# Where in a step the transpose of a finished attention output is issued

## The chip, the cores and the metric

The kernel runs on one core of a Trainium2 chip. The metric is the time of one execution on the device, in microseconds; lower is better. One core has TensorE (matrix products and transposes, into PSUM banks), VectorE, ScalarE, GpSimd and SyncE, which here issues all the DMAs. Each engine works through its own queue in order.

## What is computed

One layer of an encoder on 1024 tokens of width 1024, in 32-bit floats:

```python
h = rmsnorm(x)
[qA|kA|vA|qB|kB|vB|gA|gB] = h @ w_in
yA = differential attention (4 heads, rotary, block-causal mask), each head's output normalised
yB = chunked band attention (8 heads, own chunk and 8 before, learned bias)
x += (sigmoid(gA) * (yA @ w_up_a) + sigmoid(gB) * (yB @ w_up_b)) @ w_out
x += cross-attention to 256 memory tokens (4 heads)
x += SwiGLU(rmsnorm(x)); out = rmsnorm(x)
```

The change touches the attention phase alone, that is `yA`, `yB` and the gate products `gA`, `gB` that are mixed into it.

## The kernel before

Each product is made of three matmuls on split operands (a high and a low part): lines 217, 218 and 219 for the dense products that are mixed into the attention, lines 95 to 97 where a product stands alone. A split is a ScalarE cast (line 76) and a VectorE subtraction (line 81).

**The feed.** The dense products of the phase (the projections of queries, keys and values of later heads, and 32 gate jobs) lie in a queue, `feed`. A gate or query/key job is eight portions, each of three 512-wide matmuls and entered at 0.65 us; a value job is eight portions of three 256-wide matmuls, entered at 0.33. `feed.fill(us)` takes whole portions from the queue until their entries have used up `us`; `feed.need` runs jobs that must be done. A gate job ends with a ScalarE copy (line 257) and a store (line 258). What is left in the queue behind the attention is run by `feed.drain()`, after the loads of the next stage's operands have been issued.

**The attention.** There are 64 units: 32 of A (head `hi` 0 to 3, eight row blocks `b` each) and 32 of B (`hi` 4 to 7, two halves `c` of four block pairs `j` each). `s()` of a unit makes its scores (lines 312, 313) and softmax; it is called one unit ahead. A unit is then worked off in groups of up to four 128-wide blocks, one group in a step; there are 120 steps, 48 in A, 72 in B. A step fills, transposes the group's probabilities into the bank `tr` (A line 352, B line 438; `tr` has one buffer), splits them into `pt` out of that bank, and then multiplies the previous group's `pt` by V (`avs`, lines 366 and 367 in A, 454 in B). The last group's `avs` of a unit also finishes its output: in A it is normalised into `o`, in B added into `yt` (line 463).

**The end of a unit.** Two steps after its output is finished, `ends(2)` calls the unit's `end()`. In A that is one transpose of `o` into `tr` (line 384) and a ScalarE copy into `yt` (line 385), with a store of the whole head at the last block (line 387). In B it is only the store of a finished pair of heads (line 467).

**The next stage** loads the eight attention outputs (line 587), splits them, and multiplies by `w_up` (lines 95 to 97), gated by the sigmoid of the stored gates.

The order on each engine is laid out by the framework's planner: earlier in the program is earlier on the engine, unless the plan finds the instruction not ready and something later is.

Of the kernel before, what the change touches and what calls it, by code (L numbers as in the profile page):

```python
# [37 lines left out]
def build(tc, x, mem, wqk, wv, wg, wup, wout, wcq, wck, wcv, wco, wgu, wdn,  # L38
# [186 lines left out]
    feed = Feed()  # L225
# [4 lines left out]
    with tc.tile_pool(name="at", bufs=1, reuse_waits="tile") as at:  # L230
# [242 lines left out]
        for i in range(8):  # L473
            vj, v = vjs[i // 2]
            if i < 4:
                us = [UnitA(i, b, qks[i], v, vj) for b in range(NT)]
            else:
                us = [UnitB(i - 4, c, j, qks[i], v, vj) for c in range(2) for j in range(4)]
# [49 lines left out]
        def flush():  # L528
            nonlocal pend
            if pend:  # L530
                un, g, pt = pend
                pend = None
                un.avs(g, pt)
                if g == un.groups()[-1]:
                    ended.append((step, un))
# [3 lines left out]
        def ends(age):  # L539
            while ended and step - ended[0][0] >= age:  # L540
                ended.pop(0)[1].end()

        for n, (hi, u) in enumerate(flat):
            if u is heads[hi][0] and hi < 7:
                feed.first(*qks[hi + 1].jobs)
            if n + 1 < len(flat):
                nx = flat[n + 1][1]
                feed.need(*nx.pre_s)
                nx.s()
            if u is heads[hi][0] and hi % 2 == 0 and hi > 0:  # L550
                flush()
                feed.first(*vjs[hi // 2][0])
            gs = u.groups()
            for i, g in enumerate(gs):
                us = (FA if hi < 4 else FB) * u.weight / len(gs)
                step += 1
                feed.fill(us)
                ends(2)
                pt = u.tr(g)
                flush()  # L560
                if i == 0:
                    feed.need(*u.pre_t)
                pend = (u, g, pt)
# [699 lines left out]
```

## Time and profile before

| | us |
|---|---|
| median of three timed runs | 1790.8 (1789.49 to 1791.02) |
| the profiled execution | 1787.65 |
| its span, first to last instruction | 1785.8 |
| TensorE busy | 1743.1 |
| VectorE busy | 1085.4 |
| ScalarE busy | 765.6 |
| GpSimd busy | 516.0 |

The attention phase with the feed runs from about 76 to 645 us. A row of a view gives busy times, or for a single instruction its start and duration in us; a bracket at the end of a row tells how long the engine stood idle before it, and for what. TensorE counts as busy from a matmul's start to its modelled end, so busy times of pipelined matmuls overlap.

### The profile page before, as it was taken

The numbers are of one execution on the slowest core, as the hardware profiler recorded it, in microseconds if no ns is written. First come the engines' busy times: TensorE is split into PE (matmuls) and PEld (weight loads), VectorE is DVE, ScalarE is ACT, GpSimd is POOL, SyncE is SP. The second block draws the span as 40 slices with busy tenths as digits, with TensorE's granted clock in tenths as the row PEclk, the third lists the DMA queues.
The fourth block names the chain that finished last, engine by engine and source line by source line (L and its number), as shares of the span: only waits on it lengthen the run. The fifth ranks groups of instructions, "written<-read, shape, count | busy, mean of one in ns | idle before, by whom it ended". The sixth has DMA issues, their size and how long they took to land.

```text
span 1785.8 us, 23577 instructions
## 1 busy us (share of the span) xinstructions
PE 1743.1 (98%) x8836; PEld 1469.2 (82%) x8836; DVE 1085.4 (61%) x1497; ACT 765.6 (43%) x1425; POOL 516.0 (29%) x553
## 2 busy tenths in 40 slices
PE   7999999999999999999999999999999999999997
PEld 7778797898898888888888887778888888888886
DVE  6585666656766644435645545886676656655556
ACT  5354554545545544213542334453333333334343
POOL 3231213213323201200000001476766655400002
PEclk9999999999999999999999999999999999999999
DMA  5331313212222256412331113315645434587664
GB/s 193 103 93 66 102 47 104 65 60 61 68 85 63 76 195 233 156 62 86 116 118 49 58 59 135 125 71 195 253 163 191 165 142 174 215 283 193 195 192 139
DMA packets 75729, 229.79 MB, mean 129 GB/s; under 512 B 9184, under 2 KB 9440, under 8 KB 71776
## 3 DMA queue, kind: packets, MB, share of 16 engines
q1 hardware_dynamic: 75616, 228.30, 37.8%
q8 instruction: 69, 1.13, 0.3%
q14 instruction: 44, 0.36, 0.1%
HBM read 160.10 MB, written 55.57 MB: 121 GB/s over the span
## 4 chain that ended last, share of the span: by engine, by line
PE 65%; issue 3%; DVE 3%; ACT 1%; POOL 1%; DMA 1%; DVEq 0%; POOLq 0%; ACTq 0%
PE bk L903 11%; PE bk L904 11%; PE bk L902 11%; PE acc L217 5%; PE acc L218 5%; PE acc L219 5%; PE s L96 2%; PE s L95 2%; PE s L97 2%; PE s L217 2%; PE s L218 2%; PE s L219 2%; PE av L454 1%; PE tr L438 1%; PE av L95 0%
## 5 line engine op out<-in xcount | busy, mean ns | idle before, releaser
L218 PE MATMUL acc<-t,wsp 128*128 128x512 f32 (+1 forms) x704 | 270.5, 384 | 0.0
L217 PE MATMUL acc<-t,wsp 128*128 128x512 f32 (+1 forms) x704 | 270.5, 384 | 0.0
L219 PE MATMUL acc<-t,wsp 128*128 128x512 f32 (+1 forms) x704 | 270.4, 384 | 0.0
L902 PE MATMUL bk<-T,w 128*128 128x512 f32 x616 | 240.0, 390 | 2.2 <-ACT r L990 2.0
L903 PE MATMUL bk<-T,w 128*128 128x512 f32 x616 | 239.8, 389 | 1.3 <-DVE w L897 1.3
L904 PE MATMUL bk<-T,w 128*128 128x512 f32 x616 | 239.8, 389 | 0.4 <-DVE T L897 0.4
L897 DVE TENSOR_TENSOR w<-fr,w 128x512 fp32r<-128x512 f32 x132 | 142.9, 1115 | 69.5 <-ACT w L896 69.1
L81 DVE TENSOR_TENSOR wsp<-raw,wsp 128x1024 fp32r<-128x1024 f32 x98 | 122.1, 1246 | 74.1 <-ACT wsp L76 72.9
L76 ACT CAST wsp<-raw 128x1024 fp32r<-128x1024 f32 x96 | 100.7, 1049 | 124.8 <-PE s L219 50.2
L219 PEld LDWEIGHTS acc<-t,wsp 128*128 128x128 f32 x704 | 133.3, 189 | 25.2
L218 PEld LDWEIGHTS acc<-t,wsp 128*128 128x128 f32 x704 | 133.3, 189 | 23.0 <-DVE wsp L81 0.8
L217 PEld LDWEIGHTS acc<-t,wsp 128*128 128x128 f32 x704 | 133.3, 189 | 22.2
L897 DVE TENSOR_TENSOR do<-dr,do 128x1024 fp32r<-128x1024 f32 x77 | 96.5, 1260 | 78.3 <-ACT do L896 76.1
L902 PEld LDWEIGHTS bk<-T,w 128*128 128x128 f32 x616 | 115.6, 188 | 26.6 <-ACT r L990 2.4
L903 PEld LDWEIGHTS bk<-T,w 128*128 128x128 f32 x616 | 115.6, 188 | 25.5 <-DVE w L897 1.7
L904 PEld LDWEIGHTS bk<-T,w 128*128 128x128 f32 x616 | 115.6, 188 | 25.0 <-DVE T L897 0.9
L896 ACT CAST do<-dr 128x1024 fp32r<-128x1024 f32 x77 | 81.0, 1053 | 112.6 <-PE bk L904 98.6
L903 PE MATMUL bk<-do 128*128 128x512 f32 x308 | 120.0, 390 | 2.5 <-DVE do L897 2.5
L904 PE MATMUL bk<-do 128*128 128x512 f32 x308 | 119.8, 389 | 0.0
L217 PE MATMUL acc<-wsp,t 128*128 128x256 f32 (+1 forms) x368 | 118.3, 321 | 1.0 <-POOL wsp L80 1.0
L902 PE MATMUL bk<-do 128*128 128x512 f32 x308 | 119.0, 389 | 0.0
L219 PE MATMUL acc<-wsp,t 128*128 128x256 f32 (+1 forms) x368 | 116.8, 318 | 0.7 <-DVE wsp L81 0.7
(218 smaller groups left out, 3728.9 us busy)
## 6 DMA issues: line engine op xcount, KB each, us to landing
fr<-in_wgu SPq DMA_DIRECT2D x44, 512.0 KB, 5.3
ad<-r SPq DMA_DIRECT2D x22, 512.0 KB, 3.3
sd<-s SPq DMA_DIRECT2D x11, 1024.0 KB, 4.1
dw<-in_wdn SPq DMA_DIRECT2D x22, 512.0 KB, 5.4
wd<-dw SPq DMA_DIRECT2D x11, 1024.0 KB, 3.9
dr<-sd SPq DMA_DIRECT2D x44, 256.0 KB, 3.7
dr<-wd SPq DMA_DIRECT2D x44, 256.0 KB, 3.9
dr<-ad SPq DMA_DIRECT2D x33, 256.0 KB, 5.0
```

Of the source, the lines that this page charges most:

```text
L76: act.copy(out=hi, in_=src)
L81: lo_eng.tensor_tensor(out=lo, in0=src, in1=hi.bitcast(F32), op=ALU.subtract)
L95: pe.matmul(acc, lh, rh, start=(i == 0), stop=False)
L96: pe.matmul(acc, ll, rh, start=False, stop=False)
L217: pe.matmul(acc, lh, rh, start=(i == 0), stop=False)
L218: pe.matmul(acc, ll, rh, start=False, stop=False)
L219: pe.matmul(acc, lh, rl, start=False, stop=(i == n - 1))
L896: self.act.copy(out=hi, in_=src)
L897: self.dve.tensor_tensor(out=lo, in0=src, in1=hi.bitcast(F32), op=ALU.subtract)
L902: mm(acc, l[0], r[0], start=start, stop=False, skip_group_check=onto)
L903: mm(acc, l[1], r[0], start=False, stop=False, skip_group_check=onto)
L904: mm(acc, l[0], r[1], start=False, stop=stop, skip_group_check=onto)
```

## The change

The budget of a step's fill is handed out in two halves, and `ends(2)` stands between them.

```diff
                 us = (FA if hi < 4 else FB) * u.weight / len(gs)
                 step += 1
-                feed.fill(us)
+                feed.fill(us / 2)
                 ends(2)
+                feed.fill(us / 2)
                 pt = u.tr(g)
                 flush()
```

The budget is `FA` (5.5) or `FB` (3.8) times the unit's weight, over its number of groups. For A the weight is 0.3 + 1.2 (b + 1) / 8, for B 0.5, 0.9, 1.3 and 1.3 by `j`. The loop that it is given to:

```python
        def fill(self, us):
            while us > 0 and self.q:
                us -= self.step()
```

## Rows read from the trace of the kernel before

**Rows 1.** The page, part 1: busy us, share of the span, instructions.

```profile
PE 1743.1 (98%) x8836; PEld 1469.2 (82%) x8836; DVE 1085.4 (61%) x1497; ACT 765.6 (43%) x1425; POOL 516.0 (29%) x553
```

**Rows 2.** Stretches: length, then each engine's busy us, clock, DMA.

```profile
76.00:392.00 316.00, 307.18 (x1713) 262.83 (x1712) 208.85 (x423) 162.77 (x409) 79.52 (x135) 0.99 0.25 77
392.00:644.55 252.55, 249.01 (x1533) 218.03 (x1532) 163.99 (x317) 133.88 (x292) 74.21 (x124) 1.00 0.22 70
644.55:671.62 27.07, 27.07 (x122) 22.37 (x120) 12.41 (x11) 12.99 (x16) 0.00 (x0) 1.00 0.80 288
```

**Rows 3.** TensorE's waits in A and B: total us, times, longest us.

```profile
PE tr L352 <- ACT yt L385: 4.9, 7, 1.7
...
PE tr L438 <- DVE pt L81: 2.9, 5, 0.9
```

**Rows 4.** One end in order of time (TensorE and ScalarE): start, duration, instruction.

```profile
254.69 0.27 PE L384 MATMUL tr<-ident,o 128*128 128x128 f32 x1
255.49 0.26 ACT L385 COPY yt<-tr 128x128 f32<-128x128 f32 x1
255.80 0.66 PE L352 MATMUL tr<-ident,pp 128*128 128x128 f32 x4 [0.36 <-ACT yt L385]
```

**Rows 5.** Line 384, what its engine idled for before it: us, times.

```profile
  DVE pt L81: 0.4, 2
```

**Rows 6.** Last two groups, in order of time: transposes, and the subtract that frees the bank.

```profile
639.11 0.62 PE L438 MATMUL tr<-ident,pb 128*128 128x128 f32 x4
640.43 0.69 DVE L81 TENSOR_TENSOR pt<-tr,pt 128x512 fp32r<-128x512 f32 x1 [0.96 <-ACT pt L76]
642.24 0.49 PE L438 MATMUL tr<-ident,pb 128*128 128x128 f32 x3
643.32 0.56 DVE L81 TENSOR_TENSOR pt<-tr,pt 128x384 fp32r<-128x384 f32 x1 [2.20 <-ACT pt L76]
```

**Rows 7.** Line 218 on TensorE by stretch: length, busy us (matmuls), clock.

```profile
606.38:644.55 38.17, 13.35 (x34) 1.00 0.16 56
633.39:636.24 2.85, 1.17 (x3) 1.00 0.00 0
644.55:671.62 27.07, 15.57 (x40) 1.00 0.80 288
```

**Rows 8.** VectorE's groups, 606.38 to 644.55: times, busy us, mean ns, idle before.

```profile
L417 DVE TENSOR_TENSOR pb<-s,bt 128x640 f32<-128x640 f32 (+2 forms) x6 | 4.2, 747 | 0.2 <-PE s L313 0.2
L418 DVE TENSOR_REDUCE mx<-pb 128x1 f32<-128x640 f32 (+2 forms) x6 | 4.2, 739 | 0.0
L463 DVE TENSOR_TENSOR yt<-av,o 64x256 f32<-64x256 f32 x5 | 2.1, 413 | 0.1
```

**Rows 9.** From the last attention product to the first up product, all engines.

```profile
644.03 0.52 PE L454 MATMUL av<-pt,v 128*128 128x256 f32 x3
645.69 0.77 SPq L467 DMA_DIRECT2D yb<-yt  x1
648.91 1.74 SPq L587 DMA_DIRECT2D t<-ya  x4
652.66 1.05 ACT L76 CAST t<-t 128x1024 fp32r<-128x1024 f32 x1 [1.08 <-DMA t<-ya]
663.65 2.35 DVE L81 TENSOR_TENSOR t<-t 128x1024 fp32r<-128x1024 f32 x2
671.62 0.39 PE L95 MATMUL s<-t,wsp 128*128 128x512 f32 x1
```

**Rows 10.** Two places where TensorE stood idle, columns as in Rows 2.

```profile
304.00:308.00 4.00, 2.03 (x11) 1.22 (x9) 2.75 (x7) 3.72 (x9) 1.50 (x3) 1.00 0.66 229
308.40:312.20 3.80, 3.80 (x11) 2.96 (x11) 3.05 (x8) 2.01 (x7) 0.93 (x3) 0.55 0.87 248
1112.00:1116.00 4.00, 2.35 (x12) 1.33 (x12) 4.00 (x5) 3.05 (x5) 1.21 (x2) 1.00 0.89 358
1116.00:1120.00 4.00, 3.85 (x23) 2.89 (x22) 3.41 (x6) 1.19 (x2) 0.65 (x1) 1.00 0.19 78
```

## The prediction, before the changed kernel was run

> **What bounds the kernel now.** I start with the page's busy times: TensorE is busy 1743.1 of 1785.8 us [rows 1], so the time is TensorE's fixed work plus its idle time, and a change that only reorders can act on idle time alone. Cutting the attention phase into stretches gives that idle time: 316.00 - 307.18 = 8.8 us in the four heads of A, 252.55 - 249.01 = 3.5 us in the four of B, and none in the 27.07 us behind the last attention product [rows 2]. The list of TensorE's waits names it. In A the largest is the one the edit aims at: the next transposes wait 4.9 us in 7 places for the copy out of the shared transpose bank; in B it is 2.9 us in 5 places for the subtract that empties that bank [rows 3].
>
> One such stall in order of time: TensorE transposes the finished output at 254.69, ScalarE comes to copy the result only at 255.49, and TensorE idles 0.36 us ahead of the transposes at 255.80 [rows 4]. Between them the planner had already slipped in the products with V, so most of the copy was covered.
>
> **What the edit removes.** At most those 4.9 us, out of 32 finished outputs. I take 4.0: the copy then has half a fill, some 2 us, to get through ScalarE, which covers all but the longest waits.
>
> **What it moves, and what each costs.** The 32 transposes and copies are the same instructions. Is the output ready half a fill earlier? Ahead of the 32 transposes TensorE idled only 0.4 us, for the subtract that frees the bank, never for the output itself [rows 5]. The end transpose now asks for that bank half a fill after the previous group. Group, cast and subtract of one step take 2.01 us with four cells (639.11 to 641.12) and 1.64 with three (642.24 to 643.88) [rows 6]; half a fill is about as long, and the previous products with V come on top. Bounds: 0 and 32 times the 0.58 us that one B wait took (2.9 / 5, [rows 3]), 18 us, if nothing is slipped in; I take 0.5, by the 0.4 of [rows 5], since the planner does slip products into such holes [rows 4]. The stores of a head's output (four of A, three of B) go half a fill earlier on SP's queue, ahead of the second half's gate stores and weight loads. A load stuck behind one would be late by the copy's wait; weights are asked for one job ahead (eight 0.65 portions, over 5 us), and this is hidden. I cost it, and the copy's new place on ScalarE's queue among gate copies, at nothing; if that cover were gone it would be the same 4.9 us again.
>
> **What it changes without saying so: how much the fill hands out.** The fill loop takes whole portions until its budget is used up, so it overshoots by part of one. A portion of 0.65 is three 512-wide matmuls. In a B step with budget 1.65 the old call takes three portions; two calls with 0.82 take two each, four in all (so too for B's 1.71 and 1.90). The trace agrees on the three: between the transposes at 633.39 and 636.24 line 218, once per portion, ran 3 times [rows 7]. For A the same arithmetic gives 7 to 8 portions (budget 4.12), 5 to 6 (2.89), and no change for 2.47, 3.30, 3.71 and 4.95: five more in a head of 12 steps. The jobs are a finite queue. Before, about 41 portions are left over behind the last step: 40 of line 218 in the 27.07 us there [rows 7]. Number the steps 1 to 120, 48 of A and 72 of B. At step n the new code has taken about 20 + (n - 48) portions more, and the old one still had 41 + 3(120 - n). These meet at n = 107; walking through the calls with V's portions of 0.33 gives 109. So the queue runs dry in the first group of head 7's unit (c 0, j 3). Steps 110 to 120 have no filler, and nothing is left behind the attention. The total of dense work is the same; its cover moves from where it was needed to where it wasn't.
>
> **Cost 1, the eleven bare steps.** Before, steps 109 (606.38) to the last product with V (644.55) took 38.17 us, of which 34 portions at 27.07 / 40 = 0.677 us were 23.0 [rows 7]. TensorE's own attention work there is 15.2 us. Bare, the single transpose bank sets the pace: by the code's groups, eight with three cells at 1.64 and four with four at 2.01, 21.2 us, and 0.67 from the last bank's release to the last product, 21.8. That is the lower end: 21.8 - 15.2 = 6.6 us idle. VectorE also has the softmax and output work of these units, 4.2 + 4.2 + 2.1 = 10.5 us [rows 8]; if none of it fits beside the bank's cycle, the stretch is 32.3 and the idle time 17.1. Two facts pull in opposite directions: VectorE stands free for about two thirds of each cycle, but its scores and the subtracts arrive in lumps of 0.8 us. I take the middle, 12.
>
> **Cost 2, the way into the next stage.** The last product with V ends at 644.55, and SP stores the output at 645.69; the load of the first operand is only issued at 648.91; its cast starts at 652.66, ends about 653.7, and the last operand's subtract starts at 663.65 and ends near 666.0 [rows 9]. Before, this was covered by the 27.07 us of left-over portions, and the up product began at 671.62 with every operand ready. Without them TensorE has nothing from 644.55 to 653.7: 9.2 us, the lower end. Then it runs at the pace of the operands: 12.3 us until 666.0, in which the 48 matmuls of the first up column, 10.8 us at 0.677 for three, fit; 1.5 idle, and about 1 more until the first gate pair has been loaded and a bank comes free. Sum 11.7; I take 12. The upper end adds a repeated wait for the gates (3) and a return to full clock (1.3, below): 16.
>
> **Clock.** After 304 to 308, where TensorE was busy 2.03 of 4.00 us, it was granted 0.55 of the full clock from 308.4 to 312.2, the lower of its two levels (1.2 instead of 2.4 GHz) for nearly all of it; after 1112 to 1116, 2.35 of 4.00, it kept 1.00 [rows 10]. Eleven matmuls took those 3.80 us, at 0.226 they would have taken 2.5: 1.3 us for one return. I take 1.0, after the 9 us gap, where most of it hides behind operands that aren't there yet.
>
> The Trainium skill ("TensorE: Matmul & The Clock Gate", section "Why this matters for your kernels") warns of idle gaps between bursts of matmuls, after which the clock is back at its lower level. [...]
>
> **Sum.** -4.0 (stall) -1.0 (part of B's 2.9, as four portions between groups outlast the bank's cycle) +0.5 (bank) +12 +12 +1.0 = +20.5. Against the profiled execution's own 1787.65 us (span 1785.8) this gives 1808.2. That execution lies 3.15 under the median 1790.8 of the timed runs; on the scale of the median I forecast **1811**, 1.1% slower.
>
> **The rivals.**
> 1. *Only the stall goes* (faster). The order on each engine is the planner's. If it lets dense portions slip past steps whose weights or bank aren't ready in its plan, some 20 us or more of them still stand behind the last attention product and cover the loads; then the result is 4.9 us off, 1786, at most 7.8 off with B's waits. It decides at a left-over of about 20 us, the 645 to 666 that the operands need. Against it: the old trace follows the call order exactly (3 portions per step, 40 left, [rows 7]). 5%.
> 2. *Cold attention* (slower still). At the lower level the 15.2 us of attention work becomes 30.4, over the 27 I expect of the bare stretch, and each group takes 0.4 longer in the bank's cycle, 12 times: +5; with the return in full and a second one, +27 in all, 1787.65 + 27 + 3.15 = 1818. For it, 304 to 308; against it, 1112 to 1116 [rows 10]. 20%.
> 3. *Cheap depletion.* Both lower ends, 6.6 + 9.2, less 7.8 of stalls, is +8: 1799. If the planner also finds products of the next stage to start in the last head, the sum comes within 0.2% of before. 4% for within 0.2%; the rest of this case belongs to the forecast's lower tail.
>
> **How the numbers follow.** Forecast 71%, cold 20%, cheap to nothing 4%, only the stall 5%. The range goes from the sum of the lower ends, 1799, to the cold case with half of cost 1's and cost 2's upper margins, 1828. An upper sum of everything (17.1 + 16 + 5 + 3) is 1832 and is left out. A measurement of this kernel can tell about 0.2% (3.6 us) from no change. Slower 0.91, same 0.04, faster 0.05.
>
> **What would show it.** In the new profile: four of line 218 between B's transposes; the last gate copy (line 257) by the middle of head 7 rather than behind the attention; gaps of TensorE ahead of transposes waiting on the pt subtract or pb scaling in the last head; a hole of 9 us or more ahead of the first up matmul (lines 95 to 97), released by ScalarE's cast of an operand; the wait of line 352 on line 385 at under 1 us. TensorE's busy time stays near 1743 while the span grows by about 20. It is wrong if portions of lines 217 to 219 still stand between the last line 454 and the first line 95, or if the hole there is short.

## The result and the profile after

The changed kernel takes 1818.2 us (1816.65 to 1820.96), the kernel before 1790.9 in the same series: a ratio of 1.0157, 95% interval 1.0142 to 1.0172. Forecast were 1811 and a range of 1799 to 1828, slower. The profiled execution took 1817.23 us with a span of 1815.4, 29.6 above the span before.

TensorE's busy time on the page, which answers to [rows 1]:

```profile
PE 1751.1 (96%) x8836; PEld 1474.3 (81%) x8836; DVE 1090.3 (60%) x1497; ACT 769.0 (42%) x1425; POOL 516.6 (28%) x553
```

The number of instructions is the same. Of the 29.6 us, 8.0 are in busy time (matmuls that last longer, or overlap less with others) and the rest is idle time. Line 218 on TensorE by stretch, as in [rows 7] (length, busy us, count, clock, DMA): a B step, then from step 109's transposes to the last product with V.

```profile
645.35:650.08 4.73, 1.57 (x4) 1.00 0.44 151
660.67:689.08 28.41, 0.00 (x0) 0.88 0.08 29
```

A B step now hands out four portions, and from step 109 (its transposes begin at 660.67, before at 606.38) there is not one left. The same stretches with all engines, as in [rows 2]: filled steps, bare steps, and from the last product with V to the end of the first up column (48 matmuls of lines 95 to 97).

```profile
76.00:660.67 584.67, 566.38 (x3248) 490.88 (x3248) 360.18 (x705) 290.67 (x677) 145.79 (x244) 0.99 0.24 76
660.67:689.08 28.41, 21.58 (x113) 16.03 (x111) 19.03 (x37) 14.30 (x32) 7.23 (x15) 0.88 0.08 29
689.08:711.86 22.78, 14.30 (x48) 10.44 (x49) 11.44 (x10) 13.14 (x13) 0.00 (x0) 0.70 0.86 338
```

Since the dense work has only moved, each stretch can be compared with its own work. Before, 34 + 40 portions, 50.1 us at 0.677, stood behind step 109's start; now they stand ahead of it.

| stretch | before, without these portions | after | lost |
|---|---|---|---|
| up to step 109 | 606.4 + 50.1 = 656.5 | 660.7 | 4.2 |
| bare steps | 38.2 - 23.0 = 15.2 | 28.4 | 13.2 |
| to the end of the first up column | 48 x 0.2267 = 10.9 (671.62 to 682.50) | 22.8 | 11.9 |

The sum, 29.3, is all but 0.3 of the difference of the spans. The way into the next stage, in order of time, answers to [rows 9]:

```profile
688.45 0.63 PE L454 MATMUL av<-pt,v 128*128 128x256 f32 x3 [0.21 <-DVE pt L81]
689.96 0.32 SPq L467 DMA_DIRECT2D yb<-yt  x1
692.71 1.74 SPq L588 DMA_DIRECT2D t<-ya  x4
696.43 1.05 ACT L76 CAST t<-t 128x1024 fp32r<-128x1024 f32 x1 [6.94 <-DMA t<-ya]
697.52 0.80 PE L95 MATMUL s<-t,wsp 128*128 128x512 f32 x1 [8.45 <-ACT t L76]
...
711.63 0.39 PE L97 MATMUL s<-t,wsp 128*128 128x512 f32 x1
```

The chain from the last product to the first up matmul is the same, store, load, cast; it took 8.4 us, where before the first cast ended 9.2 us after the last product. What is missing is the work that ran meanwhile. TensorE's waits (total, times, longest), as in [rows 3]:

```profile
PE s L95 <- ACT t L76: 8.4, 1, 8.4
PE tr L438 <- DVE pt L81: 8.3, 12, 0.9
...
PE tr L384 <- DVE pt L81: 3.8, 2, 2.1
PE s L312 <- POOL qst L297: 2.8, 1, 2.8
PE tr L352 <- DVE pt L81: 2.6, 1, 2.6
...
PE tr L352 <- ACT yt L385: 1.7, 2, 0.9
```

The wait that the edit aims at fell from 4.9 to 1.7 us. Three others came up in its place within the same heads: the end transpose waits for a bank still being emptied (line 384, 3.8, before 0.4), the next group for that bank (2.6, before 0.3), scores for queries (2.8, before 0.9). From A's first group to B's first group TensorE stood idle for 12.5 us (79.35 to 402.60), before 8.8 (79.63 to 382.45); from there to step 109 for 5.8, before 3.5. That is 5.9 us more; the busy time grew by 48.4 (566.38 - 518.02), 1.7 less than the 50.1 reckoned for the portions, which leaves the 4.2 of the table.

### The profile page after: what moved, and what is told of

Same layout as the page of the kernel before. It is cut to its first block, busy times and chain, and to the rows that moved or that the text cites. A ratio compares the mean times of both kernels' runs of the same rounds, so it can differ in the third digit from the quotient of the medians.

```text
span 1815.4 us, 23551 instructions
## 1 busy us (share of the span) xinstructions
PE 1751.1 (96%) x8836; PEld 1474.3 (81%) x8836; DVE 1090.3 (60%) x1497; ACT 769.0 (42%) x1425; POOL 516.6 (28%) x553
## 4 chain that ended last, share of the span: by engine, by line
PE 81%; DVE 7%; issue 4%; ACT 3%; POOL 2%; DMA 2%; SPq 0%; DVEq 0%; POOLq 0%; ACTq 0%
PE bk L904 10%; PE bk L905 10%; PE bk L903 10%; PE acc L218 9%; PE acc L219 9%; PE acc L217 9%; PE s L97 2%; PE s L95 2%; PE s L96 2%; PE av L454 2%; PE s L219 2%; PE s L217 2%; PE s L218 2%; PE tr L438 1%; PE s L312 1%
```

## The experiments

In all of them the base is the kernel before.

**The place alone.** The second half of the fill gets what the first half left of the budget, so a step hands out what it did.

```diff
             while us > 0 and self.q:
                 us -= self.step()
+            return us
...
-                feed.fill(us)
+                us = us / 2 + feed.fill(us / 2)
                 ends(2)
+                feed.fill(us)
```

> The end transpose stands in the middle of the fill as in the change, but the second half's budget is lessened by what the first half overshot, so that a step hands out exactly as many portions as the kernel before (3 in a B step) and some 41 stay behind the attention. If the loss of the change comes from the amount handed out, this is near the kernel before: the copy's stall goes (up to -4.9 us), new waits on the transpose bank come (the changed kernel's trace shows 3.8 us in 2 places at line 384), so 1787 to 1796 us, with some 27 us of gate matmuls ahead of the first up matmul. If the place of the transpose itself costs, by blocking the single transpose bank in mid-step, it is 1805 us or more.

Measured 1789.3 us against 1789.5, ratio 1.0000 (0.9991 to 1.0008). The left-over is back, 40 of line 218 behind the last product with V:

```profile
645.16:672.20 27.04, 15.42 (x40) 1.00 0.80 287
```

TensorE's waits in A's heads (lines are one higher here):

```profile
PE av L367 <- DVE o L373: 4.0, 2, 2.3
PE tr L385 <- DVE pt L81: 3.9, 2, 2.1
PE tr L353 <- ACT yt L386: 3.4, 4, 1.4
PE s L313 <- ACT pp L337: 2.0, 1, 2.0
PE s L313 <- POOL qst L298: 1.6, 1, 1.6
```

The copy's wait shrinks from 4.9 to 3.4 and two new ones of 4 us stand beside it. TensorE's idle time in A even rose, to 13.1 us (80.12 to 383.53); against that, its granted clock was 1.00 over that stretch, where the kernel before ran at 0.55 from 308.4 to 312.2 [rows 10]. What the edit is about is worth nothing measurable, and it costs nothing either: the loss of the change is the amount.

**The amount alone.** Two half fills, both ahead of the end.

```diff
-                feed.fill(us)
+                feed.fill(us / 2)
+                feed.fill(us / 2)
                 ends(2)
```

> The fill is called twice with half the budget, as in the change, but both calls stand ahead of the end transpose, which stays where it was. If the amount is the cause, nearly the whole loss is here: eleven bare steps (13 us in the changed kernel's trace) and an uncovered way into the next stage (12 us), 1812 to 1820 us, with the hole of 8 us or more ahead of the first up matmul. If the place is the cause, this is 1791 us.

Measured 1822.6 us, ratio 1.0182 (1.0168 to 1.0196): the whole loss and a little more than expected. The hole is there, and line 352 now waits 9.9 us for the copy:

```profile
PE tr L352 <- ACT yt L385: 9.9, 8, 2.7
PE s L95 <- ACT t L76: 8.6, 1, 8.6
```

Against the kernel before in its own series this is 33.0 us, and the change 27.3. That the new place helps with this amount is therefore likely, but not shown: the two intervals overlap (1.0168 to 1.0196, 1.0142 to 1.0172), and the trace of this run has TensorE at 0.50 of its clock without a break from 678.7 to 706.0, longer than the change has at a time.

**The uncovered way alone.**

```diff
-        feed.fill(F0)
+        feed.fill(F0 + 26.65)
```

> The kernel before, with the 41 portions that it leaves behind the attention worked off ahead of its first step (first fill 29.65 instead of 3); each step hands out what it did, and the queue lasts to the last step. This is the second cost alone, the uncovered way into the next stage. If it is what the changed kernel's trace shows (first up column ends 22.6 us after the last product with V, of which 10.9 are work), 1800 to 1805 us. If the operands' loads would be hidden by something else, 1791.

Measured 1802.4 us, ratio 1.0070 (1.0056 to 1.0084), 12.9 us over its 1789.5. The first up matmul comes after 10.5 us of idle time, and the next ones are spaced 0.4 to 0.7 us instead of 0.23:

```profile
671.71 0.53 PE L454 MATMUL av<-pt,v 128*128 128x256 f32 x3
682.73 0.79 PE L95 MATMUL s<-t,wsp 128*128 128x512 f32 x1 [10.50 <-ACT t L76]
683.32 0.63 PE L96 MATMUL s<-t,wsp 128*128 128x512 f32 x1
```

**Unfilled steps with jobs behind them.**

```diff
-                feed.fill(us)
+                if step < 110:
+                    feed.fill(us)
```

> The kernel before, with no fill in steps 110 to 120; those 33 portions join the 41 behind the attention, so that the way into the next stage stays covered. This is the first cost alone. By the changed kernel's trace (28.4 us from step 109's transposes to the last product with V, of which 15.2 are work) 1802 to 1806 us; by the bank's cycle alone (6.6 us) 1797; if bare steps cost nothing 1791.

Measured 1793.4 us, ratio 1.0019 (1.0009 to 1.0029): 3.9 us, between the bank's cycle alone and no cost at all. The reason is in line 218 by stretch, from step 109 to the last product with V and behind it:

```profile
606.09:635.93 29.84, 7.16 (x18) 1.00 0.08 28
635.93:675.00 39.07, 21.63 (x56) 1.00 0.78 269
```

18 portions run in steps that ask for none (step 110 on): the planner took them from the left-over into the holes. This run therefore does not show the cost of a bare step; it shows that a step is bare only when the queue is empty. My expectation overlooked that.

**Bare steps and nothing behind them.**

```diff
-        feed.fill(F0)
+        feed.fill(F0 + 45)
```

> The kernel before, its steps and places unchanged, with the first fill raised by 45, so that the queue is empty from step 110 on and nothing is left behind. Against the run with the left-over alone moved up front (1802.4 us) the difference is the bare steps with no later portions for the planner to slip in. If these cost what the changed kernel's trace shows (28.4 - 15.2 = 13 us), 1813 to 1818 us. If bare steps cost as little as with a left-over behind them (3.9 us), 1806 us.

Measured 1813.4 us, ratio 1.0137 (1.0124 to 1.0150). The uncovered way cost 12.9; this adds 11.0 for the bare steps. Waits over the whole run:

```profile
PE s L95 <- ACT t L76: 8.4, 2, 8.1
...
PE tr L438 <- DVE pt L81: 7.0, 11, 1.0
```

The transposes' wait for their bank is 7.0 us in 11 places, where the kernel before has 2.9 in 5 [rows 3]. The profiled execution, 2.7 us above the median, has 12.7 us of loss in the bare steps, 12.8 behind them and 3.0 ahead of step 109 (table in the next section). With the portions per step and the end's place untouched, an empty queue alone costs 24.4 us of the change's 27.3.

**Another bank for the end's transpose,** at the old place and then in mid-fill with unchanged portions.

```diff
-                tr = tr_tile()
+                tr = acc_tile()
                 pe.transpose(out=tr[:, :P], in_=self.o[:, 0], identity=ident)
```

> The kernel before, with the end transpose written into one of the two banks of the dense products instead of the transposes' single bank. The next step's transposes no longer share a bank with the copy, so the 4.9 us of line 352's waits for it should go: 1784 to 1788 us, if that shared bank is the stall. If the dense products then wait for the copy in its place, no change from 1789.5 us.

> End transpose in mid-fill, portions per step as in the kernel before, and the transpose in a bank of the dense products. If the place alone brought nothing because the transpose met the transposes' bank still in use (3.9 us in 2 places), that wait goes and this is 1784 to 1788 us, as with the old place. If dense banks are held up in mid-fill, 1789 to 1793 us.

Measured 1793.5 us at the old place, ratio 1.0025 (1.0016 to 1.0034), and 1790.4 in mid-fill, 1.0005 (0.9997 to 1.0014). At the old place both expectations missed: no gain, and 4.4 us slower. In mid-fill it came out as for dense banks held up. The wait of line 352 for the copy is gone from both lists. In mid-fill a dense product waits for it instead (line 218, 2.1 us in 2 places). At the old place, in A's heads, these stand in its place:

```profile
PE s L312 <- ACT pp L336: 3.6, 2, 2.0
PE s L312 <- POOL qst L297: 2.9, 1, 2.9
PE tr L352 <- DVE pt L81: 2.7, 2, 1.5
PE acc L384 <- ACT r L286: 2.0, 2, 1.1
PE av L366 <- DVE o L372: 1.9, 1, 1.9
```

**Half a left-over.**

```diff
-        feed.fill(F0)
+        feed.fill(F0 + 13)
```

> The kernel before with the first fill raised by 13, so that some 17 to 20 portions, 12 to 14 us, are left behind the attention. The loads need some 9 us to the first operand and 21 to the last. If a left-over of 20 us is needed, 3 to 6 us are lost, 1793 to 1796 us; if the first up column's own work hides the later operands, only the first 9 us need cover and this is 1789 to 1791 us.

Measured 1794.5 us, ratio 1.0029 (1.0018 to 1.0040): 5.4 us. 16 portions are left, 10.8 us, and the first up matmul follows them without a hole:

```profile
660.71:671.90 11.19, 6.24 (x16) 1.00 0.78 277
671.71 0.50 PE L95 MATMUL s<-t,wsp 128*128 128x512 f32 x1
```

The first up column then ends at 686.07, 14.4 us for 10.9 of work: it runs at the pace of the operands and loses some 3.5 there. The number is in the range expected for a needed left-over of 20 us. Its waits of line 352 for the copy also doubled, as in the amount alone:

```profile
PE tr L352 <- ACT yt L385: 10.4, 12, 1.9
```

Yet this execution lost nothing up to step 109 (table in the next section) and 3.7 us in the first up column. That is the whole of the 3.8 us by which its 1791.4 lies above the 1787.65 of the profiled execution before; it was the fastest of seven, and the rest of the 5.4 between the medians is in no trace.

**The copy on VectorE,** at the old place and in mid-fill with unchanged portions.

```diff
-                act.copy(out=yt[:, self.b * P:(self.b + 1) * P], in_=tr[:, :P])
+                dve.tensor_copy(out=yt[:, self.b * P:(self.b + 1) * P], in_=tr[:, :P])
```

> The kernel before, with the end's copy on VectorE instead of ScalarE; place, bank and portions as before. If the 4.9 us stand for a copy that is late because ScalarE is in an Exp, line 352's waits for it fall under 2 us; if that wait is a time that can be collected, 1784 to 1787 us, and if other waits take its place, as with the transpose in mid-fill (1789.3) and in another bank (1793.5), 1788 to 1794 us.

> End transpose in mid-fill, portions per step as in the kernel before, the copy on VectorE. Neither the copy's stall nor ScalarE's queue should matter here; the transposes' bank can still be in use in mid-fill. If the waits in A's heads only change places, 1787 to 1793 us; if each of them counts, 1784 us or less.

Measured 1797.7 us, ratio 1.0043 (1.0030 to 1.0057), and 1796.2, 1.0036 (1.0023 to 1.0048). Both miss: TensorE waits longer for VectorE's copy than for ScalarE's. Waits in A's heads, first at the old place, then in mid-fill:

```profile
PE tr L352 <- DVE yt L385: 12.0, 11, 2.9
```

```profile
PE tr L353 <- DVE yt L386: 7.9, 5, 3.6
PE s L313 <- POOL qst L298: 2.9, 1, 2.9
```

The stall of [rows 4] is not ScalarE's alone. Not all of the loss need be this wait: the trace of the old place has TensorE at 0.50 of its clock from 99.2 to 106.0 and from 314.2 to 317.6, that of mid-fill from 106.6 to 113.4 and from 294.4 to 301.2, the kernel before in A only around 310 [rows 10]. Why VectorE comes later is not shown.

## Why the prediction was right, and where it was not

**The count of the fill was the right step,** and it carried the sign. Four portions in a B step, an empty queue at step 109, no portion behind the attention, the last gate copy (line 257) at 660.9: all as counted. Three signs came out otherwise: the hole is 8.4 us and not 9 or more, line 352 waits 1.7 us for the copy and not under 1, and TensorE's busy time rose by 8.0 instead of staying. The place alone gave 1.0000, the amount alone 1.0182, an empty queue without either 1.0137.

**Cost 1, the bare steps:** taken 12, bounds 6.6 and 17.1. The trace shows 13.2, the runs 11.0 (1813.4 - 1802.4). The mechanism named, the single bank of the transposes, is there: of the 6.8 us that TensorE stood idle in these steps (28.41 - 21.58), 4.4 in 7 places are waits for it. The other 6.4 us are busy time (21.58 against 15.2): the attention's matmuls no longer overlap dense ones, and some ran at the lower clock. How much each of these makes is not shown. Here are three of the waits (TensorE in order of time):

```profile
665.09 0.55 PE L438 MATMUL tr<-ident,pb 128*128 128x128 f32 x3 [0.82 <-DVE pt L81]
...
673.74 0.55 PE L438 MATMUL tr<-ident,pb 128*128 128x128 f32 x3 [0.65 <-DVE pt L81]
...
677.66 1.11 PE L438 MATMUL tr<-ident,pb 128*128 128x128 f32 x4 [0.86 <-DVE pt L81]
```

**Cost 2, the way into the next stage:** taken 12 and 1.0 for the clock; the trace shows 11.9, the run 12.9.

**The step that failed is the filled part.** I put it at -4.0 - 1.0 + 0.5 = -4.5 us. The trace shows +4.2, and these 8.7 us are about the distance from the 20.5 summed to the 29.6 of the two spans. In its own terms, TensorE's idle time ahead of step 109 was to shrink and grew, by 3.6 us in A and 2.3 in B. Two terms were wrong.
- *What the edit removes.* I took 4.0 of the copy's 4.9 us as a gain. That wait did go down, by 3.2 in the changed kernel, but the place alone gained 0.0 (within about 0.1%, 1.6 us). A wait is not a sum to be collected: in these runs, where this one shrank, TensorE ran into others (lines 384, 352 and 312 in the change, 367 and 385 in the place alone). The other bank shows the same: the wait gone, no time gained. The +0.5 for the transposes' bank belongs here; it was 3.8, in two places only, between my bounds and nearer the lower.
- *What more portions cost.* I counted them as free cover wherever they run, and even took 1.0 for B's shorter waits. With four portions to a step, B's wait for the bank was not shorter ahead of step 109, 3.9 us instead of at most 2.9:

```profile
PE tr L438 <- DVE pt L81: 3.9, 5, 0.9
```

The amount alone is 9.1 us above the run with an empty queue and unchanged steps (1822.6 - 1813.4), though that one loses the same two covers. How the filled part fared in each run can be reckoned as in the first table: the start of step 109, less the 606.4 of before and 0.677 for each portion that ran earlier than before. Each row is one execution.

| run | step 109 begins | portions moved ahead of it | lost up to there | bare steps | up column | line 352's wait for the copy |
|---|---|---|---|---|---|---|
| the change | 660.7 | 74 | 4.2 | 13.2 | 11.9 | 1.7 |
| the amount alone | 663.7 | 74 | 7.2 | 14.8 | 11.7 | 9.9 |
| bare steps and nothing behind them | 658.1 | 72 | 3.0 | 12.7 | 12.8 | 6.6 |
| the uncovered way alone | 634.2 | 40 | 0.7 | -0.1 | 13.9 | 8.0 |
| half a left-over | 622.7 | 24 | 0.0 | -0.1 | 3.7 | 10.4 |

The two covers cost within about 2 us the same in every run that loses them; the filled part differs more. The copy's wait does not tell its loss: 10.4 us of it went with none, 1.7 with 4.2. In the last three rows some 2 us are made good ahead of A, where the portions moved to the front leave TensorE idle for 11.8 to 12.0 us instead of 13.8. Another thing that differs is the clock. In A the changed kernel had two stretches at the lower level:

```profile
301.00:304.40 3.40, 3.40 (x10) 2.74 (x10) 0.85 (x2) 0.00 (x0) 0.00 (x0) 0.50 0.73 174
321.50:324.90 3.40, 3.40 (x14) 3.04 (x13) 1.18 (x5) 1.14 (x6) 0.00 (x0) 0.50 0.75 235
```

The kernel before had one there [rows 10], half a left-over none. At the 1.3 us that the prediction reads for one return, this is an estimated 1 us or so. Why the waits came out as they did stays open: no run here held the order of the dense portions, or the clock, fixed.

**The rivals.** That only the stall goes, with portions slipping behind the attention, did not happen. But the planner does move portions: forward into holes, 18 of them where steps asked for none. It moves them when something is left to be moved. Cold attention came in part. The clock by stretch of the changed kernel (columns as in [rows 10]):

```profile
660.67:676.00 15.33, 11.64 (x68) 8.64 (x67) 12.49 (x25) 8.84 (x20) 4.72 (x10) 1.00 0.15 53
676.00:684.00 8.00, 6.39 (x28) 4.96 (x26) 4.34 (x10) 4.06 (x10) 2.20 (x4) 0.57 0.00 1
690.00:695.00 5.00, 0.00 (x0) 0.00 (x0) 0.00 (x0) 0.00 (x0) 0.00 (x0) 0.51 0.47 175
697.50:703.50 6.00, 5.94 (x12) 3.57 (x13) 5.47 (x5) 4.54 (x5) 0.00 (x0) 0.50 1.02 409
```

Full clock for the first 15 us of the bare steps, the lower level for most of the next 8, and again from the hole to 703.5. A bare stretch bound by a cold TensorE would have taken 30.4 us at least; it took 28.4 at a mean clock of 0.88, which is the lower level for a quarter of it, so the clock was not its bound, though it had a part in it: four transposes took 1.11 us at 677.66 and 0.66 at 684.59. That the cold rival's time, 1818, is the measured one is luck: it wants 17 us in the bare steps, which lost 13.2, and no loss in the filled part. The third rival, an empty queue that is cheap, puts 6.6 + 9.2 = 15.8 us on the two covers; the empty queue alone measured 24.4. The 12 matmuls up to 703.5 took 6.0 us, 2.7 at full clock; but the casts of the first four operands began at 696.43, 697.64, 699.30 and 700.56, 1.4 us apart, and three matmuls took 1.5, so most of it is hidden, as supposed. The Trainium skill's rule on idle gaps between bursts ("TensorE: Matmul & The Clock Gate", section "Why this matters for your kernels") agrees with the hole of 8.4 us (0.51 in it, 0.50 behind it). The gaps of the bare steps, 0.3 to 0.9 us, are shorter than those that it speaks of, and the clock stayed at 1.00 for the first 15 us and then fell all the same.

**The range.** Its upper end does not follow from its own sentence: 1818 with half of the two upper margins (2.6 and 2.0) is 1823, and not 1828. The measured 1818.2 lies below either.

## What to carry to other kernels

A loop that hands out whole portions until a budget is used up gives out more when the budget is split, so splitting a call is a change of amount; count it, and count when the queue runs empty, before thinking about the place. Left-over filler isn't waste: it covers the loads at the next stage's entry and is what a planner draws on for holes, so the price of an empty queue (24 us here) is that of all covers it gave. A wait in a list is not yet time to be gained: taken away by a new place or another bank, the 4.9 us here gained nothing, and other waits took their place.

## What had not been expected of the hardware

The granted clock did not follow the gaps at once: TensorE was busy 11.64 of 15.33 us with waits in most groups and kept 1.00, then fell to 0.57 for 8 us at nearly the same busy share (6.39 of 8.00, where each matmul lasts longer). VectorE, with 61% of the span busy against ScalarE's 43% [rows 1], is here the worse place for a copy of 0.27 us that TensorE waits for: 9 us over 32 copies (1797.7 against 1788.8), of which a part not separated goes with the lower clock.
